# SSM tiles turned by 32-partition block copies on ACT and POOL, and SSM products in halves of 64 columns, in a one-layer hybrid decoder step

## The chip, the cores and the metric

The kernel runs on one core of one Trainium2 chip. The metric is the device time of one execution in microseconds (us); less is better. Five engines take part, each working through its own instructions in order: PE (TensorE, matrix products; its weight loads are shown apart as PEld), DVE (VectorE), ACT (ScalarE), POOL (GpSimd) and SP, which here only issues transfers. Engines wait for one another by semaphores.

## The reference, cut to what matters

The reference computes one step of a one-layer decoder for 256 prompt positions and 8 x 4 sample positions, 288 columns in all, with 2048 features in float32: a SwiGLU half-layer, a mixer, and another SwiGLU half-layer. The mixer projects the normed input, and gives one part to a state space model (SSM) and one to attention with a window of 128. What the change touches is the SSM:

```python
bu = jnp.einsum('blgc,gpc->blgp', u32.astype(jnp.complex64), B_bar)
bu = bu.at[:, 0].add(lam_bar * h0)
a = jnp.broadcast_to(lam_bar, bu.shape)
_, h = lax.associative_scan(_ssm_combine, (a, bu), axis=1)
y = jnp.einsum('blgp,gcp->blgc', h, Cc).real + D.astype(f32) * u32
y = jax.nn.gelu(y)
y = y * jax.nn.sigmoid(jnp.einsum('blgc,gcd->blgd', y, w_glu.astype(f32)))
```

There are 64 groups (`g`) of 16 channels (`c`) with 64 complex states (`p`) each. Beside the outputs of the layer, the last states and the keys and values are returned. Attention norms its queries by their mean square over a head of 64 features.

## The kernel before, in words

**Weights.** All large products stream their weights through one list of pieces (class `Weights`). A piece holds eight blocks of 128x128 weights (fewer in the down products). SP loads it (`raw`, five buffers), ACT casts it to a high part (`wh`, L122, three buffers), DVE subtracts to get the low part (`wl`, L123), and PE makes three matmuls a block: high by high, high by low, low by high (`mm3`, L288 to L290). Loads run five pieces ahead of PE in the order of the code, casts and subtractions two.

**Slots.** Everything else is filled in between pieces. One piece is one slot: `W.next()` first emits the cast and the subtraction of the piece two slots on, then its load-ahead, then the functions that were put at this slot, in the order in which they were put there, and after that the piece's matmuls follow. `W.at(slot, f)` puts a function at a slot; `W.spread(slot, gen)` runs a generator one step a slot, each later step going to the end of the next slot's list; with `last=True` the first step also goes to the end of its slot's list. Each engine runs what it is given in this order and waits for what it needs. Slots in this document count from the mixer's first piece. Two pieces make one 128-column projection: the first is a key tile, then come eight tiles of SSM input, another key tile, two of values, and eight of queries.

**Memory.** Tiles come from pools with a number of buffers by name (`bufs=`). A tile that finds no free buffer waits for the last use of the tile that had it, also where that use comes later in the order of the code, on another engine.

**The SSM.** One tile j is 128 channels (8 groups) by 288 columns. The 288 columns are four phases (index `j` in the rearrangements, one for each position modulo 4) of 72 columns: 8 sample streams and 64 chunks of the prompt. A chunk is four positions, and the scan runs over the 64 chunks. For that the tile is needed with another layout: 4 phases x 32 channels on the 128 partitions, and (4 blocks of 32 channels) x 72 on the columns. The 128 partitions of the evicted projection hold 4 blocks of 32 channels, its columns 4 phases of 72. So the change of layout swaps the block of partitions with the phase, as a whole block of 32x72 each.

For each tile, by function: `ssm_evict` (DVE, L756) brings the projection out of PSUM into a tile `t1`. `ssm_u_store` and `ssm_u_load` change the layout through memory: one store of 128x288 from ACT's queue, four loads from SP's queue. `ssm_load_a`, `ssm_load_r` and `ssm_load_b` load the tile's matrices (`ma`, rotations `rot`, `mb`), which were computed into memory during the first half-layer. `ssm_state` is a generator of four steps: 8 products of 128x128 by 72 in float32 (two PE instructions each, L790) and four rotations on DVE (L796 to L799); then sums and two scans on DVE (L802 to L808); then two copies of the initial state on ACT (L812, L813), two products on POOL (L815, L816) and two on DVE (L817, L818); then a difference and a sum on DVE (L820, L821) that read what POOL made, and two copies on POOL (L823). `ssm_decay` writes the factor of the scan (ACT L777, POOL L778). `ssm_out` is 12 float32 products (L830 to L832), followed by the GELU on ACT (L834). `ssm_y_store` and `ssm_y_load` bring the result back to the first layout, with four stores from ACT's queue and one load on SP's queue, which loads the weights of the GLU (`gl`) behind it. `ssm_glu` has one product (L851) and a tanh on ACT; in the next slot L856 on DVE, which reads `yn`; in the next the high part and the squares on ACT (`y_split`); and in the next the low part on DVE (L741) and the sum of squares on POOL (L745).

Which slot each of these has is in the loop below the functions: tile j had its state products in slot 2j + 9, its output products in slot 2j + 14 and its GLU product in slot 2j + 18. In the same slots stand the norm of the keys (`k_norm`, slots 5 to 10 and 22 to 27), the values (`v_rows`) and the attention. `q_square` and `scores` make the mean squares of the queries: products of 128x128 by 2 columns (L1003), then the score products (L1013); `probs_t` transposes the probabilities (L1032), `pv` multiplies them with the values in halves of 64 columns (L1045).

Of the kernel before, what the change touches and what calls it, by code (L numbers as in the profile page):

```python
# [10 lines left out]
F32 = mybir.dt.float32  # L11
# [6 lines left out]
P = 128  # L18
# [19 lines left out]
SLOPES = [float(np.float32(2.0 ** (-8.0 * (h + 1) / NH))) for h in range(NH)]  # L38
MAGIC = 1.5 * 2.0 ** 23
# [649 lines left out]
def mix(tc, nc, io, es, W, base, e):  # L689
# [29 lines left out]
    ud = [dr.tile([P, N], F32, name="ud%d" % j) for j in range(8)]  # L719
    yd = [dr.tile([P, N], F32, name="yd%d" % j) for j in range(8)]  # L720
# [37 lines left out]
    def ssm_u_store(j):  # L758
        put(ud[j], UE.pop(j))

    def ssm_u_load(j):
        U[j] = sm.tile([P, 4, W1], F32, name="U", bufs=4)
        src = ud[j].rearrange("(q c) (j t) -> j c q t", q=4, j=T)
        for jr in range(T):
            get(U[j][32 * jr:32 * jr + 32], src[jr])
# [9 lines left out]
    def ssm_decay(j):  # L775
        D0[j] = sa.tile(c4, F32, name="d0", bufs=2)
        act.copy(D0[j], e["e4"][:, 4 * j:4 * j + 4, None].to_broadcast(c4))  # L777
        pool_e.memset(D0[j][:, :, 0:1], 0.0)  # L778
# [5 lines left out]
    def ssm_state(j):  # L784
        ma, u, rot = MA.pop(j), U[j], ROT.pop(j)
        b = []
        for i in range(2):
            ps = aux()
            for q in range(4):
                pe.matmul(ps[:, q * W1:(q + 1) * W1], ma[:, i, q], u[:, q], start=True, stop=True)  # L790
            b.append(ps[:, :N].rearrange("p (q t) -> p q t", q=4))
# [33 lines left out]
    def ssm_out(j):  # L825
        mb, u, cs = MB.pop(j), U.pop(j), CS.pop(j)
        ps = aux()
        for q in range(4):
            o = ps[:, q * W1:(q + 1) * W1]
            pe.matmul(o, mb[:, 0, q], u[:, q], start=True, stop=False)  # L830
            pe.matmul(o, mb[:, 1, q], cs[:, 0, q, :W1], start=False, stop=False)  # L831
            pe.matmul(o, mb[:, 2, q], cs[:, 1, q, :W1], start=False, stop=True)  # L832
        YG[j] = sm.tile([P, 4, W1], F32, name="yg", bufs=1)
        act.activation(YG[j].rearrange("p q t -> p (q t)"), ps[:, :N], AF.Gelu_apprx_tanh)  # L834

    def ssm_y_store(j):
        yg = YG.pop(j)
        dst = yd[j].rearrange("(q c) (j t) -> j c q t", q=4, j=T)
        for jr in range(T):
            put(dst[jr], yg[32 * jr:32 * jr + 32])  # L840

    def ssm_y_load(j):
        YN[j] = sm.tile([P, N], F32, name="yn", bufs=2)
        get(YN[j], yd[j])
        GL[j] = sm.tile([P, P], F32, name="gl", bufs=2)
        get(GL[j], io["w_glu"][j])
# [26 lines left out]
    for j in range(8):  # L873
        s = base + 2 * j + 5
        W.at(s, ssm_u_store, j)
        W.at(s, ssm_load_a, j)
        W.at(s + 2, ssm_u_load, j)
        W.at(s + 2, ssm_decay, j)
        W.at(s + 2, ssm_load_r, j)
        W.spread(s + 4, ssm_state(j), True)  # L880
        W.at(s + 6, ssm_load_b, j)
        W.at(s + 9, ssm_out, j)
        W.at(s + 10, ssm_y_store, j)
        W.at(s + 11, ssm_y_load, j)
        W.spread(s + 13, ssm_glu(j))
    W.at(s + 8, state_done)
    W.at(s + 17, ssm_done)
    W.spread(s + 18, e["norm"](e["ones"], acc, R_ssm, 1.0 / 1024, 4 * EPS))
# [109 lines left out]
    def scores(i):  # L998
# [3 lines left out]
        for blk in range(2):  # L1002
            pe.matmul(pq[:, 2 * blk:2 * blk + 2], sq[:, 128 * blk:128 * blk + 128],  # L1003
                      bones[:, 0:128:64], start=True, stop=True)
# [123 lines left out]
    for i in range(8):  # L1128
        s = base + 2 * (12 + i) + 2
        W.at(s, q_square, i)  # L1130
        W.spread(s + 1, scores(i), True)
        W.at(s + 9, probs_t, i)
        W.at(s + 11, pv, i)
# [194 lines left out]
```

## Time and profile before

| | |
|---|---|
| time, median of 3 runs | 1881.68 us (1880.63 to 1883.83) |
| profiled execution, its own time | 1881.9 us |
| its span (first to last instruction) | 1880.1 us |
| granted TensorE clock | 1.000 |
| PE busy | 1863.0 us, 15264 matmul instructions |
| main matmuls (L288 to L290) | 14400 |
| SSM matmul instructions (L790, L830 to L832) | 320 |
| DVE, ACT, POOL busy | 1211.9, 850.6, 300.8 us |
| SSM stage in the trace | first L790 at 828.6 us, last L851 at 945.3 us |

How to read its rows: a row of the timeline has the start in us, the time taken, the engine, the line of the code, the operation, the tiles (out<-in), the shape (partitions x columns; for a matmul first the size of the weights), a count, and in brackets how long the engine sat idle before it and what ended that. Matmuls are pipelined, so the time between two starts is what one costs. A row of groups has the busy time, the mean duration in ns of one, and the idle time before. A row of the waits has who waited for whom, with the sum in us, the number of times and the longest. A float32 product of the SSM is two matmul instructions.

### The profile page before, as it was taken

How to read it: one execution, taken by the hardware profiler on the slowest of the kernel's cores; microseconds unless marked ns; L12 is line 12 of the kernel's file. 1: busy time of each engine (PE TensorE's matmuls, PEld its weight loads, DVE VectorE, ACT ScalarE, POOL GpSimd, SP SyncE). 2: the span in 40 equal slices, each digit the busy share in tenths (PEclk: the TensorE clock that was granted, in tenths of full speed). 3: DMA queues.
4: the chain of work that ended last, by engine and by line, in shares of the span. 5: the costliest groups of instructions: out<-in, count | busy, mean ns of one | idle time of the engine just before them, and what ended most of it. 6: DMA issues, size and time to landing. Idle time of an engine off the chain costs nothing.

```text
span 1880.1 us, 37660 instructions
## 1 busy us (share of the span) xinstructions
PE 1863.0 (99%) x15264; PEld 1848.9 (98%) x15264; DVE 1211.9 (64%) x1877; ACT 850.6 (45%) x1337; POOL 300.8 (16%) x450
## 2 busy tenths in 40 slices
PE   9999999999999999999999999999999999999999
PEld 8999999999999999999988999999999999999999
DVE  6677667666667755687888885555555555555555
ACT  6443444444444444643476554433444334434433
POOL 3201011000100100211468650000000000000000
PEclk9999999999999999999999999999999999999999
DMA  7555656656665665778744456556655565556555
GB/s 265 198 181 165 217 179 213 196 170 218 213 200 171 213 213 156 238 246 290 239 137 133 158 176 183 180 165 183 191 180 171 170 197 180 167 167 205 180 162 170
DMA packets 123054, 359.04 MB, mean 191 GB/s; under 512 B 22496, under 2 KB 30688, under 8 KB 121696
## 3 DMA queue, kind: packets, MB, share of 16 engines
q1 hardware_dynamic: 114672, 340.48, 57.7%
q10 hardware_dynamic: 8208, 16.16, 2.5%
q8 instruction: 119, 1.95, 0.4%
q14 instruction: 55, 0.45, 0.1%
HBM read 338.40 MB, written 20.22 MB: 191 GB/s over the span
## 4 chain that ended last, share of the span: by engine, by line
PE 93%; DVE 2%; DMA 2%; POOL 2%; ACT 1%; issue 1%; SPq 0%; ACTq 0%; POOLq 0%; DVEq 0%
PE main L290 30%; PE main L288 30%; PE main L289 30%; DVE wl L123 1%; PE main L790 0%; DMA U<-ud 0%; PE main L832 0%; PE main L831 0%; PE main L621 0%; PE main L627 0%; PE main L830 0%; ACT wh L122 0%; POOL x L1153 0%; DMA out_kT<-s 0%; DVE sm_m L969 0%
## 5 line engine op out<-in xcount | busy, mean ns | idle before, releaser
L123 DVE TENSOR_TENSOR wl<-raw,wh 128x1024 fp32r<-128x1024 f32 (+2 forms) x677 | 751.7, 1111 | 453.9 <-ACT wh L122 451.6
L288 PE MATMUL main<-xh,wh 128*128 128x288 f32 x3136 | 902.5, 288 | 1.7 <-ACT xh L214 1.2
L290 PE MATMUL main<-xh,wl 128*128 128x288 f32 x3136 | 897.8, 286 | 0.7 <-DVE wl L123 0.6
L289 PE MATMUL main<-xl,wh 128*128 128x288 f32 x3136 | 897.3, 286 | 0.9 <-DVE xl L215 0.9
L122 ACT CAST wh<-raw 128x1024 fp32r<-128x1024 f32 (+2 forms) x677 | 636.9, 942 | 505.2 <-PE main L289 352.6
L288 PEld LDWEIGHTS main<-xh,wh 128*128 128x128 f32 x3136 | 592.8, 189 | 3.5 <-ACT xh L214 1.7
L289 PEld LDWEIGHTS main<-xl,wh 128*128 128x128 f32 x3136 | 592.8, 189 | 1.9 <-DVE xl L215 1.5
L290 PEld LDWEIGHTS main<-xh,wl 128*128 128x128 f32 x3136 | 592.7, 189 | 1.7 <-DVE wl L123 0.8
L288 PE MATMUL main<-hh,wh 128*128 128x288 f32 x1664 | 477.9, 287 | 1.2 <-DVE t L1152 0.7
L289 PE MATMUL main<-hl,wh 128*128 128x288 f32 x1664 | 476.0, 286 | 0.6 <-DVE hl L741 0.6
L290 PE MATMUL main<-hh,wl 128*128 128x288 f32 x1664 | 476.0, 286 | 0.0
L288 PEld LDWEIGHTS main<-hh,wh 128*128 128x128 f32 x1664 | 314.5, 189 | 1.8 <-DVE t L1152 0.9
L289 PEld LDWEIGHTS main<-hl,wh 128*128 128x128 f32 x1664 | 314.5, 189 | 1.0 <-DVE hl L741 0.8
L290 PEld LDWEIGHTS main<-hh,wl 128*128 128x128 f32 x1664 | 314.5, 189 | 0.2 <-DVE wl L123 0.2
L362 POOL TENSOR_TENSOR s<-s,R 128x288 f32<-128x288 f32 x88 | 70.7, 803 | 1139.2 <-ACT s L361 1139.2
L371 ACT CAST hh<-h 128x288 fp32r<-128x288 f32 x88 | 38.0, 432 | 222.9 <-DVE h L370 222.9
L361 ACT ACTIVATE s<-t 128x288 f32<-128x288 f32 x88 | 39.0, 443 | 219.9 <-DVE t L360 219.9
L392 DVE SCALAR_TENSOR_TENSOR x<-main,x 128x288 f32<-128x288 f32 x128 | 58.4, 456 | 39.9 <-PE main L290 39.5
L370 DVE TENSOR_TENSOR h<-main,s 128x288 f32<-128x288 f32 x88 | 40.1, 456 | 55.9 <-PE main L290 55.6
L360 DVE TENSOR_TENSOR t<-main,R 128x288 f32<-128x288 f32 x88 | 40.1, 456 | 45.1 <-PE main L290 44.7
L372 DVE TENSOR_TENSOR hl<-h,hh 128x288 fp32r<-128x288 f32 x88 | 40.3, 458 | 43.8 <-ACT hh L371 43.8
L224 POOL TENSOR_TENSOR acc<-acc,sq 128x288 f32<-128x288 f32 x45 | 45.3, 1006 | 46.0 <-ACT sq L220 45.1
(268 smaller groups left out, 913.9 us busy)
## 6 DMA issues: line engine op xcount, KB each, us to landing
raw<-in_w_gu SPq DMA_DIRECT2D x349, 512.0 KB, 3.9
raw<-in_w_dn SPq DMA_DIRECT2D x128, 384.0 KB, 3.1
raw<-in_w_dn SPq DMA_DIRECT2D x128, 320.0 KB, 3.2
raw<-in_w_in SPq DMA_DIRECT2D x40, 512.0 KB, 4.5
raw<-in_w_out SPq DMA_DIRECT2D x32, 512.0 KB, 3.4
mats<-stage ACTq DMA_DIRECT2D x8, 1536.0 KB, 6.8
mb<-mats SPq DMA_DIRECT2D x8, 768.0 KB, 6.2
ma<-mats SPq DMA_DIRECT2D x8, 512.0 KB, 4.2
```

What stands on the lines that cost most here:

```text
L122: self.nc.scalar.copy(wh[:, :n], t[:, :n])
L123: self.nc.vector.tensor_tensor(wl[:, :n], t[:, :n], wh[:, :n].bitcast(F32), op=ALU.subtract)
L224: eng.tensor_tensor(acc, acc, sq, op=ALU.add)
L288: pe.matmul(ps, wh[:, s], woven(rh[k]), start=first and a == 0, stop=False)
L289: pe.matmul(ps, wh[:, s], woven(rl[k]), start=False, stop=False)
L290: pe.matmul(ps, wl[:, s], woven(rh[k]), start=False, stop=last and a == n - 1)
L360: dve.tensor_tensor(t1, pg[:, :N], R, op=ALU.mult)
L361: act.activation(s1, t1, AF.Silu)
L362: pool_e.tensor_tensor(s2, s1, R, op=ALU.mult)
L370: dve.tensor_tensor(halved(h), evens(pu[:, :N]), evens(s2), op=ALU.mult)
L372: dve.tensor_tensor(hl, h, hh.bitcast(F32), op=ALU.subtract)
L392: dve.scalar_tensor_tensor(x[d], ps[:, :N], 0.5, x[d], op0=ALU.mult, op1=ALU.add)
```

## The change

The turn through memory goes: `ssm_u_store`, `ssm_u_load`, `ssm_y_store`, `ssm_y_load` and their buffers in memory. In their place `turn` copies the 16 blocks of 32x72, for `u` on ACT (`ssm_turn_u`) and for `y` on POOL (`ssm_turn_y`). The GLU weights are loaded by a function of their own.

The products of `ssm_state` and `ssm_out`, and the small ones of `scores`, are cut into two halves of 64 weight columns, which write the two halves of the PSUM partitions.

The slots move. With s = 2j + 4 instead of 2j + 5: `u` is turned in slot s (s + 1 for tiles 0 and 1), the state products are in slot s + 2 = 2j + 6, the output products in s + 7 = 2j + 11, `y` is turned in s + 8, the GLU product is in s + 11 = 2j + 15, and the norm of the SSM output starts in slot 34 instead of 37. `d0` has one buffer instead of two, `yg` two instead of one; `yn` keeps two. In attention `pv` and the first step of `scores` are put at their slots ahead of `probs_t`, and `scores` no longer goes to the end of its slot.

```diff
+HALVES = (slice(0, 64), slice(64, 128))
...
-    def ssm_u_store(j):
-        put(ud[j], UE.pop(j))
-
-    def ssm_u_load(j):
+    def turn(copy, out, src):
+
+        for a in range(4):
+            for b in range(4):
+                copy(out[32 * a:32 * a + 32, b], src[32 * b:32 * b + 32, a])
+
+    def ssm_turn_u(j):
         U[j] = sm.tile([P, 4, W1], F32, name="U", bufs=4)
-        src = ud[j].rearrange("(q c) (j t) -> j c q t", q=4, j=T)
-        for jr in range(T):
-            get(U[j][32 * jr:32 * jr + 32], src[jr])
+        turn(act.copy, U[j], UE.pop(j).rearrange("p (j t) -> p j t", j=T))
...
-        D0[j] = sa.tile(c4, F32, name="d0", bufs=2)
+        D0[j] = sa.tile(c4, F32, name="d0", bufs=1)
...
-                pe.matmul(ps[:, q * W1:(q + 1) * W1], ma[:, i, q], u[:, q], start=True, stop=True)
+                for hh in HALVES:
+                    pe.matmul(ps[hh, q * W1:(q + 1) * W1], ma[:, i, q, hh], u[:, q], start=True, stop=True)
...
-            o = ps[:, q * W1:(q + 1) * W1]
-            pe.matmul(o, mb[:, 0, q], u[:, q], start=True, stop=False)
-            pe.matmul(o, mb[:, 1, q], cs[:, 0, q, :W1], start=False, stop=False)
-            pe.matmul(o, mb[:, 2, q], cs[:, 1, q, :W1], start=False, stop=True)
-        YG[j] = sm.tile([P, 4, W1], F32, name="yg", bufs=1)
+            for a, rhs in enumerate((u[:, q], cs[:, 0, q, :W1], cs[:, 1, q, :W1])):
+                for hh in HALVES:
+                    pe.matmul(ps[hh, q * W1:(q + 1) * W1], mb[:, a, q, hh], rhs, start=a == 0, stop=a == 2)
+        YG[j] = sm.tile([P, 4, W1], F32, name="yg", bufs=2)
...
-    def ssm_y_store(j):
-        yg = YG.pop(j)
-        dst = yd[j].rearrange("(q c) (j t) -> j c q t", q=4, j=T)
-        for jr in range(T):
-            put(dst[jr], yg[32 * jr:32 * jr + 32])
-
-    def ssm_y_load(j):
+    def ssm_turn_y(j):
         YN[j] = sm.tile([P, N], F32, name="yn", bufs=2)
-        get(YN[j], yd[j])
+        turn(pool_e.tensor_copy, YN[j].rearrange("p (j t) -> p j t", j=T), YG.pop(j))
+
+    def ssm_glu_load(j):
         GL[j] = sm.tile([P, P], F32, name="gl", bufs=2)
         get(GL[j], io["w_glu"][j])
...
-        s = base + 2 * j + 5
-        W.at(s, ssm_u_store, j)
+        s = base + 2 * j + 4
         W.at(s, ssm_load_a, j)
-        W.at(s + 2, ssm_u_load, j)
+        W.at(s + 1, ssm_load_r, j)
+        W.at(s + (1 if j < 2 else 0), ssm_turn_u, j)
+        W.spread(s + 2, ssm_state(j))
         W.at(s + 2, ssm_decay, j)
-        W.at(s + 2, ssm_load_r, j)
-        W.spread(s + 4, ssm_state(j), True)
-        W.at(s + 6, ssm_load_b, j)
-        W.at(s + 9, ssm_out, j)
-        W.at(s + 10, ssm_y_store, j)
-        W.at(s + 11, ssm_y_load, j)
-        W.spread(s + 13, ssm_glu(j))
-    W.at(s + 8, state_done)
-    W.at(s + 17, ssm_done)
-    W.spread(s + 18, e["norm"](e["ones"], acc, R_ssm, 1.0 / 1024, 4 * EPS))
+        W.at(s + 4, ssm_load_b, j)
+        W.at(s + 7, ssm_out, j)
+        W.at(s + 8, ssm_turn_y, j)
+        W.at(s + 9, ssm_glu_load, j)
+        W.spread(s + 11, ssm_glu(j))
+    W.at(s + 7, state_done)
+    W.at(s + 15, ssm_done)
+    W.spread(s + 16, e["norm"](e["ones"], acc, R_ssm, 1.0 / 1024, 4 * EPS))
...
-            pe.matmul(pq[:, 2 * blk:2 * blk + 2], sq[:, 128 * blk:128 * blk + 128],
-                      bones[:, 0:128:64], start=True, stop=True)
+            for hh in HALVES:
+                pe.matmul(pq[hh, 2 * blk:2 * blk + 2], sq[:, 128 * blk:128 * blk + 128][:, hh],
+                          bones[:, 0:128:64], start=True, stop=True)
...
-    for i in range(8):
-        s = base + 2 * (12 + i) + 2
+    S = [base + 2 * (12 + i) + 2 for i in range(8)]
+    for i, s in enumerate(S):
         W.at(s, q_square, i)
-        W.spread(s + 1, scores(i), True)
+        W.at(s + 11, pv, i)
+    for i, s in enumerate(S):
+        W.spread(s + 1, scores(i))
+    for i, s in enumerate(S):
         W.at(s + 9, probs_t, i)
-        W.at(s + 11, pv, i)
```

More of the change, by code (lines that the diff above doesn't have):

```diff
@@ L718, in mix @@
     Vs = mp.tile([T * NB, 256], F32, name="Vs")
-    ud = [dr.tile([P, N], F32, name="ud%d" % j) for j in range(8)]
-    yd = [dr.tile([P, N], F32, name="yd%d" % j) for j in range(8)]
     def consts():
```

## The prediction

> **What bounds the kernel now.** First the span and the busy times, then the chain of work that ended last, then PE's waits.
>
> ```profile
> span 1880.1 us, 37660 instructions
> PE 1863.0 (99%) x15264; PEld 1848.9 (98%) x15264; DVE 1211.9 (64%) x1877; ACT 850.6 (45%) x1337; POOL 300.8 (16%) x450
> PE 93%; DVE 2%; DMA 2%; POOL 2%; ACT 1%; issue 1%; SPq 0%; ACTq 0%; POOLq 0%; DVEq 0%
> PE main L790 <- DMA U<-ud: 3.0, 2, 2.0
> PE main L851 <- DMA gl<-in_w_glu: 1.4, 1, 1.4
> ```
>
> PE sets the end, so the change is worth the PE time it takes away, less the waits it puts in. The two waits behind memory round trips make 4.4 us (L851 waits for its weights because SP's queue held them behind the load of `yn`). Now the price of an SSM product, in the timeline of PE:
>
> ```profile
> 849.64 0.29 PE L289 MATMUL main<-xl,wh 128*128 128x288 f32 x1
> 849.76 0.29 PE L290 MATMUL main<-xh,wl 128*128 128x288 f32 x1
> 849.89 0.34 PE L830 MATMUL main<-U,mb 128*128 128x72 f32 x2
> ...
> 852.48 0.37 PE L288 MATMUL main<-xh,wh 128*128 128x288 f32 x1
> 852.69 0.29 PE L289 MATMUL main<-xl,wh 128*128 128x288 f32 x1
> ```
>
> A main matmul costs 0.122 us, a weight piece 24 of them, 2.94 us: one slot. The 24 instructions of `ssm_out` (12 products, two passes each) put 852.69 - 849.76 - 0.245 = 2.68 us between main matmuls, 0.112 each; the 16 of `ssm_state` make 1.79.
>
> **The halves.** PE shows halves already, in `pv` (64 columns of weights, 128 moving) and in L1116 (16 moving):
>
> ```profile
> 1018.18 0.29 PE L290 MATMUL main<-hh,wl 128*128 128x288 f32 x1
> 1018.40 0.88 PE L1045 MATMUL main<-pt,V 128*64 128x128 f32 x12
> 1019.21 0.66 PE L1032 MATMUL main<-ident,lg 128*128 128x128 f32 x4
> ...
> 1035.23 1.11 PE L1116 MATMUL main<-pc,cv 128*64 128x16 f32 x32
> 1036.27 0.39 PE L288 MATMUL main<-hh,wh 128*128 128x288 f32 x1
> 1036.50 0.29 PE L289 MATMUL main<-hl,wh 128*128 128x288 f32 x1
> ```
>
> Twelve take 0.81 us, 0.135 a pair; thirty-two take 1.04, 0.065 a pair. A 128-column instruction alone costs 0.112, so the halves of a pair run side by side. For 72 moving columns the pair lies between 0.065 and 0.135; the stream's share of the upper row, 0.135 x 72/128 = 0.076, is near the lower one, and I take 0.08. `ssm_state` becomes 1.28 us, `ssm_out` 1.92: over eight tiles 8 x (0.51 + 0.76) = **10.2 us off PE**; at 0.065 it is 15.0, at 0.135 a loss of 7.4. For `q_square` four instructions of 0.112 become four pairs of 0.08: under 0.2 us a head pair, counted as nothing.
>
> The Trainium skill (TensorEngine Tiling (Array Packing), Key Properties) says that changing the tiling mode drains the engine, which speaks against halves between full-width matmuls. The rows agree: entering costs 0.22 instead of 0.12, leaving 0.23 instead of 0.12, about 0.2 us for each of 16 blocks, 3.3 us. My 0.08 holds these edges; with no drain the sum below would come out near 1877.
>
> **The turn of u, on ACT.** Removed are one store and four loads a tile, with the waits above; added are 16 copies of 32x72 between partition blocks. Prices from ACT:
>
> ```profile
> L642 ACT COPY stage<-km 32x64 f32<-32x64 f32 x16 | 3.9, 243 | 0.2
> 838.30 0.22 ACT L812 COPY cs<-h 128x32 f32<-128x32 f32 x1
> 838.42 0.21 ACT L813 COPY cs<-h 128x32 f32<-128x32 f32 x1
> 216.96 1.17 ACT L642 COPY stage<-km 32x96 f32<-32x96 f32 x4
> ```
>
> Copies that move between partition blocks follow each other without overlap (four, of 96 and 128 columns, in 1.17), unlike L812 and L813, 0.12 apart. So 0.26 each, 4.2 us a tile; at 0.12 it were 1.9. For the first two tiles nothing hides it:
>
> ```profile
> 818.36 0.45 DVE L756 TENSOR_TENSOR t<-main,R 128x288 f32<-128x288 f32 x1
> 819.80 0.29 PE L288 MATMUL main<-xh,wh 128*128 128x288 f32 x1
> 825.80 1.05 ACT L122 CAST wh<-raw 128x1024 fp32r<-128x1024 f32 x1 [1.59 <-issue]
> ```
>
> 819.80 is the first matmul of slot 6, where `ssm_state(0)` now stands (before, slot 9). Its `u` is evicted at 818.8 and turned at 823.0: PE waits 3.2. The second turn stands in slot 7 behind that slot's cast, which waits for PE to leave slot 6 (three `wh` buffers): 1.05 + 4.2 = 5.3 after the slot's start, and `ssm_state(1)` comes 2.94 after it: 2.3 more. **5.5 us of new waits** (at 0.12 a copy, 0.9). Later turns have two slots and a state block, 7.2 us, and are hidden if DVE evicts in time.
>
> **The loops among DVE, ACT and POOL.** PE's pair of slots shrinks to 2 x 2.94 + 1.28 + 1.92 = 9.1 us, 9.6 with the GLU's 0.48. Can the others follow? The GLU product's row from the chain of waits in order of time, then DVE's queue:
>
> ```profile
> 885.46 0.48 PE main L851 x2
> ...
> 881.72 1.23 DVE L123 TENSOR_TENSOR wl<-raw,wh 128x1024 fp32r<-128x1024 f32 x1 [3.79 <-ACT wh L122]
> 882.86 0.45 DVE L856 SCALAR_TENSOR_TENSOR s<-s,yn 128x288 f32<-128x288 f32 x1
> 883.23 0.95 DVE L817 TENSOR_TENSOR cs<-ra,rot 128x256 f32<-128x256 f32 x1
> 884.98 0.41 DVE L796 TENSOR_TENSOR ra<-main,rot 128x256 f32<-128x256 f32 x1
> 886.30 0.44 DVE L915 TENSOR_TENSOR t<-main,R 128x288 f32<-128x288 f32 x1
> ...
> 889.33 0.42 DVE L820 TENSOR_TENSOR cs<-cs,ra 128x256 f32<-128x256 f32 x1
> 890.00 0.28 DVE L802 TENSOR_TENSOR h<-main,h 128x32 f32<-128x32 f32 x2
> 891.47 0.66 DVE L808 TENSOR_TENSOR_SCAN ra<-d,ra 128x256 f32<-128x256 f32 x1
> ```
>
> From start to start: split 1.14, L856 0.37, the four rotations from L796 1.32, L820 and L821 0.67, L802 to L808 2.1. With the eviction's 0.37 the first loop is: evict, ACT turns 4.2, the two state copies 0.25, the next cast 1.05, DVE splits 1.14, scans 2.1, L820 0.67: 9.8 us for two slots. In slots 12 to 15 this is 0.7 over PE's 9.1: two pairs, 1.5 us. ACT is also rid of issuing five stores a tile, which this loop doesn't hold.
>
> The second loop hangs on a wait the diff makes without saying so. `yn` keeps two buffers. `turn_y(j)` stands in the slot in which L856 of tile j-2 last reads its buffer, so from j = 2 the 16 POOL copies wait for that. Behind them on POOL stand L815 and L816 of another tile, and for those waits L820 on DVE, with the next eviction and split behind it. Its parts:
>
> ```profile
> 243.74 2.16 POOL L608 COPY rep<-bb 64x64 f32<-64x64 f32 x4
> 379.88 0.87 POOL L608 COPY rep<-bb 64x64 f32<-64x64 f32 x4
> 883.15 0.75 POOL L815 TENSOR_TENSOR ra<-ra,rot 128x256 f32<-128x256 f32 x1
> 883.87 0.91 POOL L816 TENSOR_TENSOR ra<-ra,rot 128x256 f32<-128x256 f32 x1
> 868.15 0.42 DVE L817 TENSOR_TENSOR cs<-ra,rot 128x256 f32<-128x256 f32 x1
> ```
>
> L817 takes 0.42 alone and 0.95 beside L815; four POOL copies take 0.87 alone and 2.16 where DVE's split and two more operations ran beside them. They block each other, operation by operation. Sixteen copies are 3.5 us alone and 8.6 at the crowded rate; DVE has some ten such operations in that stretch and is idle for part of it, so I take 5.7. Loop: evict, split, rotations, L856, 3.2; copies 5.7; L815 and L816 1.6; L820 and L821 0.75: **11.3 us** for two slots where PE needs 9.6. It holds for tiles 2 to 5, four pairs of slots: 4 x 1.7 = 7.0. At 3.5 the loop is 9.1 and costs nothing; at 8.6 it is 14.2 and costs 18.4.
>
> The Trainium skill (SBUF — State Buffer, SBUF: two separate sides) names the shared port pair an exclusive lock, held for a whole instruction, the loser fully blocked. L817's two durations agree. By that rule POOL gets about one copy for each DVE operation that blocks it; it speaks for the second rival below.
>
> **Elsewhere.** In attention `pv` and the small products of `scores` now stand side by side, ahead of transposes that wait for POOL:
>
> ```profile
> PE main L1032 <- POOL lg L984: 1.5, 2, 1.0
> PE main L1003 <- DVE rq_v L1068: 1.4, 1, 1.4
> ```
>
> I take 1 us off, of at most 2.9; DVE and POOL arriving late from the SSM could cost as much. One `d0` buffer makes `ssm_decay` wait on ACT for the scans of the slot before; queued behind it is the next turn. But DVE makes those scans ahead of the eviction for which that turn waits anyway: nothing.
>
> On SP's queue five loads a tile fall away, and with them what stood behind them. `rot` is asked for one slot ahead of its use, where it was asked for two slots ahead of `ssm_state`:
>
> ```profile
> rot<-mats SPq DMA_DIRECT2D x8, 256.0 KB, 4.3
> ```
>
> Landing takes 4.3 us against 2.94 a slot, but SP runs ahead of PE, its weight loads having five buffers. Nothing, if so; if SP ran level, 1.4 us a tile on DVE, within the air that the range leaves. `ma` and `mb` keep two and three slots. On POOL the 16 copies stand in front of L815, as counted; the sums of squares (`acc`) come after both and nobody on PE's path waits for them before the norm, which the diff puts three slots earlier than it was.
>
> **Sum.** From the profiled execution's 1881.9 us (median of the runs 1881.7): -10.2 - 4.4 + 5.5 + 1.5 + 7.0 - 1.0 = -1.6, **1880.3 us**.
>
> **Rivals.**
> - *The loops don't bind* (copies near 3.5 us, or DVE with more air than the sum of its operations leaves). For it: DVE is 64% busy over the span. Against: the lag from the first two turns. Then 1881.9 - 10.2 - 4.4 + 5.5 - 1.0 = 1871.8.
> - *Slower: POOL's second turn decides*, from copies of 8 us a tile on, by the crowded row or because a copy between partition blocks, which POOL nowhere makes before, costs more. -10.2 - 4.4 + 5.5 + 1.5 + 18.4 - 1.0: 1891.7.
> - *The halves don't pair* at 72 moving columns (0.135 a pair): +7.4 instead of -10.2, and no loop is longer than PE's pair of slots: 1889.4. The rows of `pv` speak against it.
>
> **Numbers.** A measurement tells 0.2%, 3.8 us, from no change. My sum's case 0.37; the loops don't bind 0.34; POOL decides 0.24; no pairing 0.05. Faster 0.34, same 0.37, slower 0.29. The range is from the first rival to the second, 1870.5 to 1892; my own case alone, with copies between 4.5 and 6.5, is 1875 to 1883.
>
> **What would show it.** Halves: 32 instructions of 128x64 in `ssm_state` within 1.3 us, main matmuls on both sides. Turns: 16 ACT copies 0.26 apart, PE waiting for ACT at `ssm_state(0)` and `(1)`, never at `U<-ud`. Second loop: from tile 2 on POOL's first copy waiting for DVE's L856, and DVE's L820 waiting for POOL's L816, evictions over 11 us apart. If DVE never waits for POOL there and evictions follow PE, the first rival is right; if PE waits at `ssm_out` for L820 by several us, the second.

## The result, and the profile after

The changed kernel takes 1899.3 us (median of four; 1896.9 to 1901.1) against 1881.7 us before (median of three; 1880.6 to 1883.8): ratio 1.0091, 95% interval 1.0071 to 1.0111. It is slower by 17.6 us, and outside the range of the prediction. A fourth execution of the kernel before took 3425.6 us and is left out. In the changed kernel the line numbers have moved: the main matmuls are L289 to L291, the copies of both turns L761, the state products L791, the output products L832, the GLU's product L847, its reader on DVE L852, the rotations L797 to L800, the scans L808 and L809, POOL's two products L816 and L817, DVE's L818, L819, L821 and L822, the eviction L755, the loads of `ma`, `rot` and `mb` L769, L773 and L782.

The head of the page after, with the chain of work that ended last:

```profile
span 1899.3 us, 38496 instructions
PE 1868.3 (98%) x15616; PEld 1848.0 (97%) x15616; DVE 1207.2 (64%) x1877; ACT 881.0 (46%) x1465; POOL 346.6 (18%) x578
PE 47%; POOL 3%; DVE 2%; issue 1%; ACT 1%; DMA 1%; SPq 0%; POOLq 0%; DVEq 0%; ACTq 0%
```

The span grew by 19.2 us in the profiled execution. All of it comes before the matmul below: its row before, quoted in the prediction behind L1116, starts at 1036.50, and the same matmul now starts 19.2 us later.

```profile
1055.66 0.29 PE L290 MATMUL main<-hl,wh 128*128 128x288 f32 x1
```

PE's waits, in total us, times, longest us. The waits for `U<-ud` and for `gl` are gone; the turn of u (L791 for ACT), the turn of y (L847 for POOL, and L832 behind it) and a load (`ma`) have taken their place.

```profile
PE main L791 <- DMA ma<-mats: 6.5, 2, 3.8
PE main L847 <- POOL yn L761: 4.0, 2, 3.0
PE main L791 <- ACT U L761: 3.7, 2, 2.3
PE main L1095 <- POOL ls L979: 2.8, 2, 1.7
PE main L832 <- DVE cs L821: 2.6, 3, 1.7
PE main L1028 <- POOL lg L979: 2.4, 2, 1.8
```

The halves, in PE's timeline (start, us, engine, line):

```profile
844.48 0.29 PE L291 MATMUL main<-xh,wl 128*128 128x288 f32 x1
...
846.58 0.29 PE L290 MATMUL main<-xl,wh 128*128 128x288 f32 x1
...
849.27 0.29 PE L291 MATMUL main<-xh,wl 128*128 128x288 f32 x1
849.49 1.22 PE L791 MATMUL main<-U,ma 128*64 128x72 f32 x32
...
850.86 0.29 PE L290 MATMUL main<-xl,wh 128*128 128x288 f32 x1
```

By the prediction's own working `ssm_out` now costs 846.58 - 844.48 - 0.245 = 1.86 us and `ssm_state` 1.35, so 8 x (0.44 + 0.82) = 10.1 us come off PE. The loss is elsewhere. First POOL's copies of y, one row a tile:

```profile
854.73 5.69 POOL L761 COPY yn<-yg 32x72 f32<-32x72 f32 x16
865.47 5.69 POOL L761 COPY yn<-yg 32x72 f32<-32x72 f32 x16
879.35 6.06 POOL L761 COPY yn<-yg 32x72 f32<-32x72 f32 x16 [3.07 <-DVE s L852]
892.68 5.99 POOL L761 COPY yn<-yg 32x72 f32<-32x72 f32 x16 [3.92 <-ACT U L761]
906.86 5.99 POOL L761 COPY yn<-yg 32x72 f32<-32x72 f32 x16 [4.61 <-DVE s L852]
919.31 6.21 POOL L761 COPY yn<-yg 32x72 f32<-32x72 f32 x16 [2.52 <-DVE s L852]
930.46 8.91 POOL L761 COPY yn<-yg 32x72 f32<-32x72 f32 x16 [1.81 <-DVE s L852]
940.19 4.40 POOL L761 COPY yn<-yg 32x72 f32<-32x72 f32 x16
```

Six of the eight take 5.7 to 6.2 us, near the 5.7 of the prediction, and from the third to the seventh tile they wait for L852, as it said (once the last thing that they waited for is put down to ACT). But from the first to the last they are 85.5 us apart, 12.2 for each of seven pairs of slots, where PE needs 9.6: the five pairs that end in a wait for L852 take 11.2 to 14.2, the first 10.7, the last 9.7. One turn of the loop on DVE, and DVE's waits for POOL ahead of the scans:

```profile
875.95 0.45 DVE L755 TENSOR_TENSOR t<-main,R 128x288 f32<-128x288 f32 x1
...
878.78 0.44 DVE L852 SCALAR_TENSOR_TENSOR s<-s,yn 128x288 f32<-128x288 f32 x1
...
885.61 0.69 DVE L808 TENSOR_TENSOR_SCAN ra<-d,ra 128x256 f32<-128x256 f32 x1 [1.42 <-POOL cs L812]
...
887.29 0.89 DVE L821 TENSOR_TENSOR cs<-cs,ra 128x256 f32<-128x256 f32 x1
...
888.43 0.45 DVE L755 TENSOR_TENSOR t<-main,R 128x288 f32<-128x288 f32 x1
```
```profile
DVE ra L808 <- POOL cs L812: 6.7, 3, 3.1
```

Eviction to L852 3.3 us, POOL's copies (third row above) to 885.4, then the scans, which wait for POOL because the zeroing of the decays stands behind the copies, then L821 and L822, and the next eviction: 12.5 us. This is the last eviction of a tile and the only one over 11 us behind the one before it; the later pairs run through the same wait without one.

And PE's clock. Two stretches of 3.4 us next to each other; the columns are the stretch, its length, busy us of PE, PEld, DVE, ACT and POOL with instructions, the granted clock, DMA share, GB/s. Then the view by cores.

```profile
870.40:873.80 3.40, 1.23 (x33) 1.18 (x33) 2.58 (x5) 2.33 (x4) 3.18 (x7) 1.00 0.37 140
873.80:877.20 3.40, 3.40 (x14) 3.40 (x15) 3.40 (x7) 1.15 (x4) 0.61 (x3) 0.50 0.61 200
```
```profile
core 0: 1899.3 us, clock 0.993
```

After a stretch in which PE was busy for 1.23 of 3.40 us, the next runs at half clock. 0.007 x 1899.3 = 13.3 us of full clock are missing over the span, where the profiled execution of the kernel before had a mean clock of 1.000. The four executions of the changed kernel had 0.993 to 0.997.

### The profile page after: what moved, and what is told of

It is laid out like the page before. It is cut to its first block, busy times and chain, and to the rows that moved or that the text cites. A ratio compares the mean times of both kernels' runs of the same rounds, so it can differ in the third digit from the quotient of the medians.

```text
span 1899.3 us, 38496 instructions
## 1 busy us (share of the span) xinstructions
PE 1868.3 (98%) x15616; PEld 1848.0 (97%) x15616; DVE 1207.2 (64%) x1877; ACT 881.0 (46%) x1465; POOL 346.6 (18%) x578
## 4 chain that ended last, share of the span: by engine, by line
PE 47%; POOL 3%; DVE 2%; issue 1%; ACT 1%; DMA 1%; SPq 0%; POOLq 0%; DVEq 0%; ACTq 0%
PE main L289 15%; PE main L290 15%; PE main L291 15%; POOL yn L761 2%; DVE wl L124 0%; DMA ma<-mats 0%; ACT wh L123 0%; POOL lg L979 0%; POOL x L1151 0%; POOL rq_o L954 0%; ACT lg L972 0%; DVE lg L1019 0%; POOL acc L744 0%; DVE sm_m L964 0%; POOL rq_t L953 0%
## 5 line engine op out<-in xcount | busy, mean ns | idle before, releaser
L289 PE MATMUL main<-xh,wh 128*128 128x288 f32 x3136 | 907.2, 289 | 1.2 <-ACT lg L1015 1.2
L291 PE MATMUL main<-xh,wl 128*128 128x288 f32 x3136 | 901.1, 287 | 0.7 <-DVE wl L124 0.6
L289 PEld LDWEIGHTS main<-xh,wh 128*128 128x128 f32 x3136 | 596.2, 190 | 4.6 <-ACT lg L1015 1.4
L291 PEld LDWEIGHTS main<-xh,wl 128*128 128x128 f32 x3136 | 596.1, 190 | 1.7 <-DVE wl L124 0.8
L289 PE MATMUL main<-hh,wh 128*128 128x288 f32 x1664 | 478.6, 288 | 0.0
L291 PE MATMUL main<-hh,wl 128*128 128x288 f32 x1664 | 476.8, 287 | 0.0
L289 PEld LDWEIGHTS main<-hh,wh 128*128 128x128 f32 x1664 | 315.2, 189 | 0.5
L291 PEld LDWEIGHTS main<-hh,wl 128*128 128x128 f32 x1664 | 315.2, 189 | 0.2 <-DVE wl L124 0.2
```

The costliest lines, as they stand in the source:

```text
L289: pe.matmul(ps, wh[:, s], woven(rh[k]), start=first and a == 0, stop=False)
L291: pe.matmul(ps, wl[:, s], woven(rh[k]), start=False, stop=last and a == n - 1)
```

## The experiments

Medians in us; the ratio is to the kernel before, measured beside each.

| run | what it is | median | ratio, 95% interval |
|---|---|---|---|
| halves_only | before, with halves in `ssm_state`, `ssm_out` | 1878.8 | 0.9979 (0.9968 to 0.9990) |
| turns_only | after, without these halves | 1898.4 | 1.0083 (1.0068 to 1.0098) |
| turn_y_last | after, POOL's copies last in their slot | 1885.7 | 1.0015 (1.0005 to 1.0024) |
| d0_on_act | after, decays zeroed by ACT | 1900.3 | 1.0095 (1.0078 to 1.0112) |
| ma_on_act | after, `ma` loaded from ACT's queue | 1898.7 | 1.0088 (1.0074 to 1.0102) |
| u_turn_alone | after, y through memory | 1881.3 | 0.9999 (0.9990 to 1.0008) |
| attention_alone | before, with the attention's part | 1884.5 | 1.0010 (1.0001 to 1.0019) |
| both_straight | after, both turns one copy each | 1868.6 | 0.9933 (0.9918 to 0.9947) |
| y_straight | after, POOL's turn one copy | 1878.8 | 0.9986 (0.9976 to 0.9995) |
| y_turn_alone | halves_only with POOL's turn of y | 1884.8 | 1.0017 (1.0007 to 1.0027) |
| y_last_old_slots | the same, copies last in their slot | 1880.5 | 0.9987 (0.9978 to 0.9996) |

**One part alone, one part undone.**

halves_only makes this edit in the kernel before, and the same in `ssm_out`; turns_only makes the reverse edit in the changed kernel.

```diff
-pe.matmul(ps[:, q * W1:(q + 1) * W1], ma[:, i, q], u[:, q], start=True, stop=True)
+for hh in HALVES:
+    pe.matmul(ps[hh, q * W1:(q + 1) * W1], ma[:, i, q, hh], u[:, q], start=True, stop=True)
```

> The kernel before with nothing changed but the products of ssm_state and ssm_out in halves of 64 columns; u and y still go through memory and every slot stays where it was. Theory (the halves give what the sum says and the loss lies in the turns): the blocks cost 1.35 and 1.85 us instead of 1.79 and 2.68, 8 x (0.44 + 0.83) = 10.2 us, so 1882 - 10.2 = 1872, between 1869 and 1876, with the two memory waits of 4.4 us still there. Rival (switching to halves and back is what costs, or lowers TensorE's clock): 1885 or more, with stretches of lower clock.

> The changed kernel with the products of ssm_state and ssm_out at full width again. Theory (POOL's copies stand in the loop of DVE and POOL, which takes 12.5 us for two slots): PE loses 10.2 us of saving, but its own two slots grow from 9.6 to 10.8 us, so that each of the four long pairs waits 1.25 us less, and fewer gaps are long enough to lower the clock: 1899 + 10.2 - 5 - 2 = 1902, between 1897 and 1908. Rival (the halves are the loss): 1882 - 4.4 + 5.5 = 1883.

1878.8 and 1898.4. Alone, the halves bring 3.6 of their 10 us, less than the theory and more than the rival had; in the changed kernel they bring nothing (1899.3 with them, 1898.4 without, within the spread of both). PE's waits in halves_only show a part of what takes the rest; L792 is its state product, L852 its GLU product:

```profile
PE main L792 <- DMA U<-ud: 3.1, 2, 2.2
PE main L852 <- DMA gl<-in_w_glu: 2.4, 2, 1.6
PE main L792 <- DVE ra L806: 1.0, 2, 0.8
```

The memory waits of before are still there or longer (3.0 and 1.4 then), since PE comes sooner and the loads don't. In the profiled execution, 5.8 us shorter than that of before (1874.3 against 1880.1), these waits are 2.1 us longer and one stretch of 3.4 us at half clock costs 1.7, most of the 4.3 that are missing there. So the halves are neither the loss nor, behind memory or a loop, a gain of their full size.

turn_y_last, d0_on_act and ma_on_act, each an edit of the changed kernel, in this order:

```diff
-W.at(s + 8, ssm_turn_y, j)
+W.at(s + 8, lambda s=s, j=j: W.at(s + 8, ssm_turn_y, j))
...
-pool_e.memset(D0[j][:, :, 0:1], 0.0)
+act.mul(D0[j][:, :, 0:1], D0[j][:, :, 0:1], 0.0)
...
-get(MA[j].rearrange("p a q m -> p (a q m)"), e["mats"][j][:, :1024])
+put(MA[j].rearrange("p a q m -> p (a q m)"), e["mats"][j][:, :1024])
```

> The changed kernel with POOL's 16 copies of a tile moved to the end of the same slot, behind the memset of the decays, the two rotations of the other tile on POOL and DVE's L852. Theory: L816 and L817 no longer stand behind the copies, so DVE's scans and L821 don't wait for them, the loads of rot are asked for in time, and evictions follow PE at 9.6 to 10 us a pair; left are the first two turns on ACT (5.5 us): 1882 - 10.2 - 4.4 + 5.5 + 1.5 - 1.0 = 1873, between 1869 and 1882, and few stretches of half clock. Rival one (ACT's turn of u and the three earlier slots are the loss): unchanged, 1895 to 1901. Rival two (copies on POOL slow DVE wherever they stand, by the shared port): 1888 to 1898.

> The changed kernel with the zeroing of the decays' first column made by ACT in place of POOL, so that it doesn't stand behind POOL's copies. Theory: the scans L808 no longer wait for POOL (6.7 us in the trace of the changed kernel), but L821 then waits for L816, which still stands behind the copies and ends about 0.5 us before L821 starts now: only 0.5 us for each of two to four pairs is regained, 1895 to 1899. Rival (the zeroing on POOL alone is the loss, L816 has air): the pairs fall from 12.5 to 11 us, 1888 to 1893.

> The changed kernel with the loads of ma (ssm_load_a) asked for on ACT's queue in place of SP's, so that they don't stand behind the load of rot, which waits for POOL. Theory (the loop of POOL and DVE is the root, the late ma its second price): PE's waits for ma (6.5 us, longest 3.8) fall away, but the loop stays at 12.5 us for two slots, so PE waits at the next step instead, for L821's cs or for yn: 1892 to 1897 against 1899. Rival one (the late load is the whole of the loss behind the sum): 1886 to 1891. Rival two (ma is late by its own landing and not by the queue): unchanged.

Moving POOL's copies behind its other work of the slot takes 13.6 us off (1899.3 to 1885.7); less than expected, since PE then waits for the copies' result instead:

```profile
PE main L847 <- POOL yn L761: 7.1, 6, 4.1
```

Neither of the two smaller suspects is worth anything alone. Without the zeroing on POOL, DVE waits at L821 for L816, which still stands behind the copies (11.2 us in four waits; 3.6 in one in the changed kernel). With `ma` on another queue its waits fell from 6.5 to 3.5 us and others rose:

```profile
PE main L847 <- POOL yn L761: 5.4, 3, 3.0
PE main L832 <- DVE cs L821: 5.3, 5, 1.7
...
PE main L791 <- DMA ma<-mats: 3.5, 1, 3.5
```

PE's waits are places where it meets the loop; closing one moves it to the next.

u_turn_alone is this edit of the changed kernel, with `ssm_glu_load` loading `yn` from memory ahead of `gl`; attention_alone is the last two parts of the change's diff, from the product with `bones` on, in the kernel before.

```diff
-W.at(s + 8, ssm_turn_y, j)
+W.at(s + 8, ssm_y_store, j)
```

> The changed kernel in all but POOL's turn of y: y goes through memory again by a store and a load, in the slots where the turn and the load of w_glu stand. Theory (POOL's turn of y is the loss): the halves' 10.2 us and the wait for u from memory (3.0) are off, the first two turns of u (5.5) with a stretch of half clock (1.7), ACT's loop (1.5) and the attention's 2 us are on: 1882 - 10.2 - 3.0 + 5.5 + 1.7 + 1.5 + 2 = 1880, between 1875 and 1885. Rival (ACT's turn of u, which waits for DVE's eviction with casts behind it, takes its share in every pair): 1888 to 1896.

> The kernel before with the attention's part of the change alone: q_square's product in halves, and pv, scores and the transposes of a slot in the changed kernel's order. Theory (the traces of the changed kernel, of the turns alone and of the turn of u alone each lose 1 to 2 us between the end of the SSM and the last pv, where the run with the halves alone loses nothing): slower by 1 to 2 us, 1883 to 1885. Rival (the prediction's step: the products side by side take 1 us off the waits for POOL and DVE): 1880 to 1881.

Both came as expected: 1881.3, and 2.0 us slower for the attention's part alone (0.2 to 3.6 by the interval; its halves and its new order together). The loss is in the turn of y as it stands in the changed kernel, and the attention's part costs time where the prediction gave it 1 us of gain.

**The turns' time taken away.**

y_straight makes this edit in the changed kernel, both_straight also the same for u on ACT; the layout isn't changed then, so what comes after has other numbers in it and the same work.

```diff
-turn(pool_e.tensor_copy, YN[j].rearrange("p (j t) -> p j t", j=T), YG.pop(j))
+pool_e.tensor_copy(YN[j], YG.pop(j).rearrange("p q t -> p (q t)"))
```

> The changed kernel with each turn replaced by one straight copy of 128x288, on ACT for u and on POOL for y; the blocks of 32 partitions are not reordered, so the output is another one. Theory (the halves' 10.2 us and the memory waits of 4.4 us arrive where no turn binds; the attention's order costs 2): 1882 - 10.2 - 4.4 + 2 = 1870, between 1867 and 1875. Rival (the halves' gain is eaten anyway, because DVE's and ACT's other work can't follow PE's shorter slots, as the 3.6 us of halves_only suggest): 1876 to 1880.

> The changed kernel with POOL's sixteen copies of a tile replaced by one straight copy of 128x288; y is not reordered, so the output is another one; the turn of u stays. Theory (the time of the copies in front of L816 and L817 is the loss): the pairs of slots fall from 12.5 to below 10 us, and left is the early lag of the turn of u: 1876 to 1882, a little under the 1881.3 of u_turn_alone. Rival (the wait for L852 by yn's two buffers, or the moved slots, hold the loop without the copies' time): 1888 to 1896.

1868.6 and 1878.8, as the theory had it. This splits the result, for this order of taking the turns away: with both turns almost free the change gains 13.4 us (1882.0 to 1868.6), the turn of u takes 10.2 of that back (to 1878.8), the turn of y 20.5 (to 1899.3). In y_straight the straight copies, same slot and same wait for L852, run from

```profile
853.60 0.42 POOL L838 COPY yn<-yg 128x288 f32<-128x288 f32 x1
...
921.79 0.58 POOL L838 COPY yn<-yg 128x288 f32<-128x288 f32 x1 [5.30 <-DVE s L852]
```

68.2 us for the seven pairs instead of 85.5. PE's eight GLU products (L847) show the whole price: they start from 863.42 to 950.64 in the changed kernel and from 862.30 to 929.03 in y_straight, 87.2 us against 66.7. So what costs is the time of the copies at their place in the slot. The wait by the two buffers of `yn` is there in both_straight too and costs nothing by itself; with the full copies behind it it was not taken away, since no run has a third buffer. The mean clock with both turns short is 1.000, in y_straight:

```profile
core 0: 1877.7 us, clock 0.999
```

**The turn of y without the turn of u.**

y_turn_alone is the first edit in halves_only, with two buffers of `yg`, one of `d0`, and `ssm_y_load` loading `gl` only; y_last_old_slots makes the second in that run, with `ssm_turn_y` at the end of its slot's list.

```diff
-W.at(s + 2, ssm_decay, j)
+W.at(s + 4, ssm_decay, j)
-W.at(s + 10, ssm_y_store, j)
+W.at(s + 10, ssm_turn_y, j)
...
-W.at(s + 11, ssm_y_load, j)
+W.at(s + 9, ssm_y_load, j)
```

> The kernel with the halves alone (1878.8) plus POOL's turn of y in place of its trip through memory, two buffers of yg, one of d0, the decays in the slot of the state; u goes through memory in the old slots, the attention is the old one. Theory (POOL's copies stand in DVE's loop whatever turns u): 1890 to 1896, DVE's scans waiting for POOL. Rival (the loss comes only with ACT's turn of u in the same loop): 1876 to 1882.

> The run y_turn_alone (halves, POOL's turn of y in the old slots, u through memory, 1884.8) with the sixteen copies last in their slot, behind L816 and L817 of the other tile, and the load of w_glu two slots earlier. Theory (the copies cost by standing ahead of L816 and L817): DVE's waits for POOL at L821 (9.3 us) and the waits for w_glu (4.1) go: 1874 to 1879. Rival (the copies cost by their time on POOL and the port shared with DVE, wherever they stand): 1881 to 1885.

1884.8 lies between theory and rival: the turn of y costs 6.0 us over halves_only (1878.8), not 20.5. Its copies, too, are 85.7 us apart from the first to the last (851.67 to 937.40), so their distance alone doesn't say what PE loses. DVE there waits for POOL at the step that the prediction named (L822 and L817 are its L820 and L815):

```profile
DVE cs L822 <- POOL ra L817: 9.3, 5, 4.0
```

In y_last_old_slots that wait is gone and 4.3 us come back (1880.5). It falls between the two expectations, and it makes two changes at once: with the copies last, the load of `gl` also comes two slots earlier, and PE's waits for `gl` (4.1 us in y_turn_alone) are gone with it. So it doesn't show alone that the place in POOL's order decides here too; in the changed kernel turn_y_last does. The full price needs the rest of the change beside the turn of y. In y_turn_alone the last eviction of a tile is at 868.12, ahead of the third tile's copies at 877.39; in the changed kernel the evictions are still in the loop at 888.43. That the turn of u and the three earlier slots tie the evictions into the same loop fits this, but no run separates these two.

**Attempts at a better version, most of them misses.**

turn_y_last_states_later is this edit of turn_y_last, with the decays at s + 3 too; order_restored moves besides the turn of y to the end of s + 9, the load of `gl` to s + 10 and the GLU to s + 12.

```diff
-W.at(s + 1, ssm_load_r, j)
-W.spread(s + 2, ssm_state(j))
+W.at(s + 2, ssm_load_r, j)
+W.spread(s + 3, ssm_state(j))
```

> The kernel with POOL's turn of y at the end of its slot, and besides ssm_state, the decays and the load of rot of every tile one slot later, so that the turn of u has a slot more. Theory (the turns of the first two tiles on ACT cost 4.3 us of waits and one stretch of half clock, 3.4 us long): 1885.7 - 4.3 - 1.7 = 1880, between 1876 and 1883; PE waits for U for less than 1 us. Rival (the later state makes cs late for ssm_out and the wait only moves there): 1884 to 1888.

> The kernel with POOL's turn of y last in its slot and the states a slot later, with the turn of y, the load of w_glu and the GLU a slot later as well, so that POOL meets the 16 copies behind L816 and L817 of the other tile again and not ahead of them. Theory (what costs is the copies' place in POOL's order ahead of L816 and L817, not the slot of the state): PE's 19.7 us of waits for cs at ssm_out fall below 5, 1877 to 1884. Rival (a state one slot nearer to ssm_out is late by itself): 1892 to 1900.

1899.9, which neither side expected, and 1896.8 after the order on POOL was restored, where the rival was right. With `ssm_state` four slots ahead of `ssm_out` instead of five, `cs` is late at every tile; in order_restored:

```profile
PE main L832 <- DVE cs L821: 16.5, 8, 6.4
```

The later state takes away PE's first waits and gives them back at the first `ssm_out`. The four steps of `ssm_state` need their slots.

u_turn_later has u_turn_alone's steps from the load of `rot` to the GLU one slot later (`ssm_out` too, so that the five slots stay); u_turn_old_attention leaves them. Both have the old attention, and put each load of `ma` ahead of that slot's load of `rot`:

```diff
-    W.at(s, ssm_load_a, j)
+for j in range(8):
+    W.at(base + 2 * j + 4, ssm_load_a, j)
```

> The kernel with the turn of u on ACT alone (y through memory), the attention in the old order, every step from the load of rot to the GLU one slot later, five buffers of U, one of yg, and each load of ma asked for ahead of the load of rot in its slot. Theory: the halves' 10.2 us and the memory wait for u (3.0) are off, the first turns cost PE less than 1 us, ma isn't late: 1868 to 1875 with at most one stretch of half clock. Rival (the loop from DVE's eviction over ACT's turn to DVE's scans, 9.8 us by the prediction's sum for 9.6 us of PE, gathers lag and SP's loads come late again): 1876 to 1882.

> The run u_turn_alone (1881.3) with the attention in the old order and each load of ma asked for ahead of that slot's load of rot. Theory (the attention's order costs 2 us, as attention_alone showed, and the one wait for ma 3.2 us stands behind the load of rot): 1875 to 1879. Rival (the wait for ma goes over into another, since PE there waits for the loop over ACT's turn): 1879 to 1881.

1883.4 (ratio 1.0006, 0.9997 to 1.0014) and 1880.7 (0.9993, 0.9984 to 1.0002). In both the load of `gl`, queued on SP behind that of `yn`, then takes the most of PE's waits (6.2 and 5.9 us): the memory trip of y binds again when PE comes sooner.

halves_through_memory makes the first edit in halves_only and loads `gl` ahead of `yn`; gap_filled makes the second in that run.

```diff
-W.spread(s + 4, ssm_state(j), True)
+W.spread(s + (5 if j < 2 else 4), ssm_state(j), True)
...
+for _ in range((5, 3)[j] if j < 2 and i == 0 else 0):
+    pe.matmul(ps[:, :N], ident, R, start=True, stop=True)
```

> The kernel before with ssm_state and ssm_out in halves of 64 columns, the load of w_glu asked for ahead of that of y in the same slot, and the first two tiles' ssm_state one slot later. Theory: of the run with the halves alone (1878.8) PE's waits for gl (2.4), for u from memory (3.1), the rotations of DVE (1.0) and one stretch of half clock (1.7) go: 1871 to 1875. Rival (the waits move to the other loads of SP's queue or to ssm_out): 1876 to 1880.

> The run halves_through_memory with PE's wait ahead of the first two tiles' ssm_state filled: five and three products of 128x288 (0.48 us each) whose result is overwritten. They fit into the waits of 3.4 and 1.8 us that stand there. Theory (PE idle for more than about half of a 3.41-us window sets the clock to half for the next window; the six of eleven runs at 1880.2 to 1885.1 with a granted clock of 0.996 to 0.997 had such a window, the four at 1878.0 to 1879.0 with 0.999 or more had none): no stretch of half clock by those gaps, all runs near 1878 to 1880, median 1879. Rival (the clock falls for another reason, or the fillers cost their own time): median 1882 to 1885.

1881.9 (0.9997, 0.9988 to 1.0006) and 1884.0 (1.0010, 1.0001 to 1.0018). Both missed: PE now waits for `yn` itself, and for u of later tiles; the fillers stood at the first two tiles, which don't wait there, and cost their own time. They say nothing for or against the clock. No version beat halves_only, which is 0.2% faster than the kernel before.

**The clock by itself.**

gaps_in_before puts this into the second SwiGLU half-layer of the kernel before, twelve times, with n from 0 to 6; it took 1957.3 and 1965.2 us, and the rows are from the first:

```diff
+pe.matmul(ps[:, :N], ident, g[0], start=True, stop=True)
+act.copy(g[0], ps[:, :N])
+for k in range(n):
+    pool_e.tensor_copy(g[1 - k % 2], g[k % 2])
+pe.matmul(ps[:, :N], ident, g[n % 2], start=True, stop=True)
```

> The kernel before with twelve gaps put into its second FFN, 18 slots apart: PE makes a product of 128x288, ACT copies it, POOL copies it on n times (n = 0 to 6, then 2 to 6 again), and PE waits for the last copy. Idle time of PE about 0.8 us plus 0.62 for each POOL copy: 0.8, 1.4, 2.0, 2.7, 3.3, 3.9, 4.5 us. Theory (a fixed grid of 3.41-us windows in each run; a window in which PE is idle for about 1.9 us or more sets the clock to half in the next): no half clock behind n = 0 and 1, always behind n = 6, by the grid's position behind n = 2 to 5; each stretch 3.41 us long, and the starts of all stretches whole multiples of 3.413 us apart. Rival (only a window without any work lowers the clock): half clock behind none of the gaps up to n = 4 (3.3 us). The Trainium skill (TensorE: Matmul & The Clock Gate, Part 1) states the rival's rule, one idle window of some 3.4 us.

The starts of all stretches of half clock lie whole multiples of 3.413 us apart, 118 to 259 of them from the first, at 868.91. On that grid the windows that hold the gaps show PE's busy time (the second number), then the clock:

```profile
1213.66:1217.07 3.41, 1.67 (x12) 1.00 0.80 267
1217.07:1220.48 3.41, 2.07 (x15) 1.00 0.44 144
1268.27:1271.68 3.41, 1.35 (x10) 1.00 0.67 209
...
1537.92:1541.33 3.41, 1.33 (x8) 1.00 0.56 142
1582.29:1585.71 3.42, 0.93 (x6) 1.00 0.70 248
1640.32:1643.73 3.41, 1.49 (x11) 1.00 0.71 259
1643.73:1647.14 3.41, 0.79 (x4) 1.00 0.45 147
```

Half clock followed the windows with 1.35, 1.33, 0.93 and 0.79 us, and not those with 1.49 or more. (Of the gap windows not shown, five with 0.72 us or less were followed by it, three with 1.57 or more were not.) The rival falls: PE had work in those windows. A gap of 3.08 us that was split over two windows (1213.66 to 1220.48) cost no clock; one of 2.08 us inside a window (at 1268.27) did:

```profile
1214.68 0.65 PE L691 MATMUL main<-g,ident 128*128 128x288 f32 x2
1218.41 0.75 PE L695 MATMUL main<-g,ident 128*128 128x288 f32 x2 [3.08 <-POOL g L694]
```

The bill closes. The span is 75.4 us longer; PE's waits at the twelve gaps are 43.5 and the added products 24 x 0.48 = 11.5, which leaves 20.4. The ten stretches of half clock last 47.8 us, worth 23.9; 7.9 us of the gaps lie inside them, where half a clock costs nothing, so 20.0 are left.

```profile
PE main L695 <- POOL g L694: 41.7, 11, 5.5
PE main L695 <- ACT g L692: 1.8, 1, 1.8
```
```profile
core 0: 1955.5 us, clock 0.988
```

## Why the prediction was wrong

By its terms, with what the runs put in their place:

| term | predicted | measured |
|---|---|---|
| halves and memory waits | -14.6 | -15.4 (both_straight, less the attention) |
| attention | -1.0 | +2.0 (attention_alone) |
| turn of u, both its terms | +7.0 | +10.2 (both_straight to y_straight) |
| turn of y, the second loop | +7.0 | +20.5 (y_straight to after) |
| sum | -1.6 | +17.3 (1882.0 to 1899.3) |

The measured terms add up by construction, from 1882.0 us for the kernel before, taken beside both_straight. They hold for this order of taking the parts away, and the attention's 2.0 was measured in the kernel before.

- **Halves: right**, 1.35 and 1.86 us for 1.28 and 1.92. Left out was a condition: the saving is paid only while PE sets the pace.
- **Turn of u: right in its parts, low in the sum.** Sixteen copies took 4.2 us, and PE waited for them at the first two tiles, 3.7 us. y_straight's profile has besides 2.6 us of waits for `cs` at L832, which both_straight's has not, and one stretch of half clock, worth 1.7; the rest of the 10.2 is not broken down by a run. Half clock followed the first of the two waits for the turn in some of the traces.
- **The failed step is the second loop: "11.3 us" for two slots, "It holds for tiles 2 to 5, four pairs of slots".** The wait by `yn`, POOL's copies ahead of L816, their 5.7 us and DVE's wait were foreseen. The loop is 12.5 us in the pair shown and up to 14.2 in the starts of the copies. The scans stand behind the copies as well (through the zeroing of the decays, which the prediction took for "nothing" because it looked only at `d0`'s one buffer on ACT), but that is not the price alone: with the zeroing on ACT the time stayed (1900.3). In the pair of 14.2 us ACT is in the loop too: ahead of 902.40 it waits 6.6 us for DVE's L910, which stands behind L821 and L822, and the cast behind that wait holds up DVE's next split. And five pairs ended in the wait, not four. The seven pairs together are 85.5 - 7 x 9.6 = 18.3 us over PE's need, 17.0 of them in these five, where 7.0 were counted (4 x 1.7 is 6.8). The turn of y alone cost 6.0 in the old slots; PE's longest waits there are others (for `gl` 4.1, for `qsq` 3.8), so that this is near 7.0 may be luck. That the two loops, which the prediction summed one by one, make one when both turns are there fits these runs, and no run shows it.
- **SP: "Nothing, if so" was wrong in the mechanism and harmless in time.** The load of `rot` does hold up SP, and `ma` behind it kept PE waiting up to 3.8 us; with `ma` on another queue the time stayed.

```profile
SPq L773 <- DVE cs L819: 26.9, 6, 6.8
SPq L773 <- POOL ra L817: 26.0, 4, 8.0
```

- **Attention: wrong sign.** PE still waits there for POOL, in both_straight too (L1028 3.0 us, L1095 2.5), so the products placed ahead of the transposes made no air. Why it became slower was not taken apart.
- **The clock was in no term.** A sum that prices a wait of PE at its length is low when half clock follows the wait. In the two profiled executions, 21.6 us apart, PE is busy for 11.8 us more in the changed kernel than in y_straight with the same 15616 instructions (1868.3 against 1856.5), which agrees with the missing clock, 13.3 - 1.9 = 11.4 (0.993 against 0.999), and it is idle for 9.8 us more. By the median clocks of all executions (0.994 and 0.998) the clock's part is nearer 8 us. So the 18.3 us above hold waits and slow running together; what the loop would have cost at full clock, with PE then waiting instead, no run tells.
- **The rivals.** "POOL's second turn decides" came nearest in time (1891.7), but not by its mechanism, copies of 8 us; the loops that don't bind (1871.8) would have been right for a turn as short as both_straight's (1868.6).

## What to carry to other kernels

A saving on the bounding engine is worth its size only if every loop beside it still fits into the shorter period; write down the loops over all engines together, with each in-order queue's whole list for the period, rather than one loop for each edit. A block of copies put at the head of an engine's slot delays all that stands behind it; the same copies at the slot's end cost 13.6 us less here. Price a wait of PE of 2 us and more with the half clock that can follow it: 1.7 us for each stretch of 3.41 us in which PE has work.

## What the runs showed of the hardware

Half clock of PE needs no idle window. Of the windows of 3.41 us that held the twelve graded gaps and began at full clock, it followed every one in which PE was busy for 1.35 us or less and none with 1.49 us or more, on a grid that is fixed within an execution. It lasted 3.41 us, or 6.83 where the gap reached 0.95 us or more into the next window. The Trainium skill (TensorE: Matmul & The Clock Gate, Part 1) describes such a free-running window of 4096 cycles, which the grid of 3.413 us agrees with, and asks for a whole idle window, which these rows don't.

The busy time of PE is not the whole condition, though. Those gaps stood between main matmuls. Where PE ran short products of the SSM and the attention, half clock also followed windows with 2.17 us (865.50 to 868.91 in gaps_in_before itself, behind a wait for u), 1.67 (985.21 to 988.62 in y_straight) and 1.98 (958.42 to 961.83 in u_turn_later), and it did not follow one with 1.42 (850.88 to 854.30 in halves_through_memory). What is counted in a window stays open.

In halves_through_memory the executions with a mean clock of 0.999 or more took 1878.0 to 1879.0 us, those with 0.996 or 0.997 took 1880.2 to 1885.1. That the grid falls differently on the same gaps from one execution to the next fits this; one trace of a kernel doesn't show it.
